# Segment sums of the SSD heads as differences of cumulated sums, in place of masked selects

## The chip, the cores and the metric

The kernel runs on one core of a Trainium2 chip. The metric is device time in microseconds (us) from the first to the last instruction with what lies around it, lower is better. Matmuls run on TensorE (PE; weight loads are listed apart as PEld), elementwise work on VectorE (DVE), ScalarE (ACT) and GpSimd (POOL); transfers are issued by SyncE (SP) unless said otherwise.

## What is computed

One layer of a hybrid block: adaLN-modulated norm, one input projection, an RG-LRU half and an SSD (Mamba-2) half, both bidirectional, an output projection with a residual, then a squared-ReLU MLP and a final norm. There are 1024 latent tokens and 256 context tokens of width 1024. The SSD half has 8 heads in 2 groups and works in chunks of 128 tokens. What matters here is the decay inside a chunk:

```python
a_cs = jnp.cumsum(A, axis=2)                      # A = dt * (-exp(a_log)), per chunk
seg_in = a_cs[:, :, :, None] - a_cs[:, :, None, :]
l_mat = jnp.exp(jnp.where(tri, seg_in, -jnp.inf))
y_diag = jnp.einsum('bclsg,bclsge,bcsgep->bclgep', cb, l_mat, X)
```

It is done once for each direction; the second direction runs over flipped tokens. In the kernel both directions share one matrix per head: entries with l >= s hold the forward decay, those below it the backward one.

## The kernel before

**Tiling.** Everything is float32 or float32r (split into a high and a low part where a product needs it). The input projection goes in 18 steps over tiles of 128 columns (`ORDER`), each step in pieces of 512, 512 and 256 tokens, each piece 8 k tiles of three products (`in_part`, lines 342 to 344). A tile framework orders the work: each engine gets a fixed list of instructions, made at build time from priorities, and semaphores do the rest. Pools hand out buffers by tag: `up` has 4 tiles of 512 columns, `gw` has 2 (`GW_N`), the heap `b` has 11 blocks of 1286 columns, the PSUM tag `a` has 2 banks.

**The segment sums.** `m_groups` is a generator that runs between the products of the projection: after each k tile of a piece of 512 tokens `in_part` takes one step of it (`tick`), from step 11 of the order (X1) on; what is left at the end of step 15 (lg1) is run off there. There are 16 groups: 8 chunks by 2 groups of four heads. For one group POOL makes four masked tiles `z` (line 777): the decays `a` of a token and head, high part and low part, forward and backward, spread over the 128 columns l and set to zero on one side of the diagonal. Four products (line 759) with strictly triangular matrices of ones, `gt_r` and `lt_r`, add them over the 128 tokens into one PSUM bank `sg`. Two `z` tiles exist, so POOL runs two products ahead at most. The generator takes 4 steps per group and 2 at the end, 66 in all of the 80 that steps 11 to 15 offer.

**What follows.** `m_group` makes `dd` on POOL (line 795, the difference of the two step sizes, masked), takes the exponential of `sg` on ACT into `gm` (lines 805 and 124, since the helper `tab` records it), then on DVE four times (dd + dt) * gm, one per head (line 807), and gm * C B^T (line 816), and stores the result to `m_dram` on SP (line 817). `dd` and `gm` are both tiles of the tag `up`. Much later `y_chunk` loads it again (line 827).

**What shares the stretch.** On DVE: the convolutions' three steps per tile (line 426), the adaLN sums (`ada2`, line 877, two per step), the low parts of the weights (line 138), gelu products (line 907). On ACT: evacuation of the projection's pieces (line 453) and of transposes (lines 622 and 624), first convolution taps (424), Silu and Gelu with loads of their tables (124). POOL also clears the pads of the convolution tiles (lines 407 to 412). After step 15 the states follow (`ssd_state`, lines 732 to 751, PSUM tag `a`).

**Set-up.** `ssd_dt` makes the step sizes and the decays `aneg`, their high and low parts (lines 688 and 689), and the cumulated sums for another purpose (`acsp`, lines 691 to 700).

Of the kernel before, what the change touches and what calls it, by code (L numbers as in the profile page):

```python
# [15 lines left out]
P = 128  # L16
# [9 lines left out]
# order of the input projection's column tiles: (kind, index)  # L26
# [11 lines left out]
# how far ahead of its place in the program the scheduler may take some work  # L38
EARLY, EARLY_W, EARLY_C, EARLY_G, EARLY_M, EARLY_L = 300, 400, 300, 50, 100, 200
EARLY_A, EARLY_B, EARLY_E, WO_E, WO_A = 100, 100, 100, 200, 200  # L40
# every N2_MOD-th tile of the second norm is modulated on VectorE, the others on ScalarE
N2_MOD = 12
# order of products 7 and 4 of the MLP's last matmul, and in the last chunk
# [4 lines left out]
# columns of the feature-major vector pack  # L48
# [3 lines left out]
# columns of the row pack  # L52
# [4 lines left out]
def kernel(  # L57
# [39 lines left out]
    y_dram = dram.tile([4, P, L], F32, name="y_dram")  # L97
    g1_dram = dram.tile([1, D], F32, name="g1_dram")
# [18 lines left out]
    gt_r = cst.tile([P, P], F32R, name="gt_r")  # L117
    lt_r = cst.tile([P, P], F32R, name="lt_r")
# [3 lines left out]
    def tab(out_, in_, func, chain=True, **kw):  # L122
        """An activation that needs its own table: these keep their order."""
# [16 lines left out]
    def softplus(out_, v, n, tmp):  # L140
        # max(v, 0) + log1p(exp(-|v|)), the logarithm as 2 atanh(w / (2 + w))
# [14 lines left out]
    with ExitStack() as mctx:  # L156
# [12 lines left out]

        def load_split(src, n, name, scale=None, row=None, nk=8):  # L170
            """k tiles of [128, n] weights as hi and lo parts; entry k gives (hi, lo)."""
# [22 lines left out]
        sil = cst.tile([P, 16], F32, name="sil")  # L194
        tab(sil, fmv[:, V_C : V_C + 16], AF.Silu)
        # per k: c_hi, cc_hi, c_lo, cc_lo; and c, cc, 0, 0 for the columns taken in float32
# [20 lines left out]
        def norm_x(g):  # L217
            lo_i, hi_i = groups[g]
            for i in range(lo_i, hi_i):
                junk = wq.tile([P, 1024], BF16, tag="gw", name=f"sq{i}", bufs=GW_N)  # L220
                act.activation(junk, xt[i][:, :D], AF.Square, accum_out=ss[:, i : i + 1])
# [43 lines left out]
        def ada1(b):  # L265
            """Shift and scale of feature tiles 2b and 2b + 1: [shift, shift, scale, scale] x (latents, context)."""
# [41 lines left out]
        # latents in two halves and the context: entry [g][k]  # L308
# [444 lines left out]
        def m_groups():  # L753
# [3 lines left out]
            def product():  # L757
# [6 lines left out]
                if d and part:  # L764
                    m_group(c, g, sg)
# [872 lines left out]
```

## Time and profile before

| | |
|---|---|
| median of 3 runs | 1209.3 us (1208.99 to 1215.41) |
| profiled execution, span | 1212.3 us; its own whole time is not given apart |
| PE, PEld busy | 1154.7 us (95%), 944.6 us (78%) |
| DVE, ACT, POOL busy | 916.9 us (76%), 648.7 us (54%), 80.8 us (7%) |

A share of busy time is an average over the span. Matmuls are pipelined, so that a matmul's busy time is longer than the time from its start to the start of the next. Where two engines use the same memory port an instruction lasts longer than alone; the shortest of a kind and its median then lie apart.

### The profile page before, as it was taken

To read this page: it belongs to the slowest core of one execution; us is meant where nothing else is said; L and a number is where in the kernel's file an instruction comes from. 1 tells how busy PE (TensorE), PEld (TensorE's weight loads), DVE (VectorE), ACT (ScalarE), POOL (GpSimd) and SP (SyncE) were. 2 spreads that over 40 slices of the span, in tenths; PEclk is the share of its full clock that TensorE was granted. 3 is DMA by queue.
4 is the path that set the end of the run, shared out by engine and by line. 5 is a ranking of instruction groups with operands and counts; after the bars stand their busy time and mean duration, and the time that the engine had idled before them with its cause. 6 is when DMAs were issued, how large, how long until landed. Compare 5 with 4: busy or idle time off the path is not lost.

```text
span 1212.3 us, 15731 instructions
## 1 busy us (share of the span) xinstructions
PE 1154.7 (95%) x5790; PEld 944.6 (78%) x5790; DVE 916.9 (76%) x1224; ACT 648.7 (54%) x1019; POOL 80.8 (7%) x120
## 2 busy tenths in 40 slices
PE   7899898998989999989899999999999999999997
PEld 2588787787767889988578777778878888888886
DVE  3775876888997698756996566656667787889996
ACT  5868377575555177527755455545574352333343
POOL 0000000004775000000000000000000000000000
PEclk9899998999999999999899999999999999999999
DMA  9621243223243256752285653545357444435403
GB/s 335 218 84 57 75 127 120 89 88 107 77 130 122 77 186 190 232 197 97 88 277 166 225 161 136 154 157 179 121 178 312 174 174 172 142 138 210 172 10 129
DMA packets 86480, 184.39 MB, mean 152 GB/s; under 512 B 8314, under 2 KB 19962, under 8 KB 82820
## 3 DMA queue, kind: packets, MB, share of 16 engines
q1 hardware_dynamic: 86404, 183.40, 44.9%
q8 instruction: 45, 0.74, 0.3%
q14 instruction: 31, 0.25, 0.1%
HBM read 133.03 MB, written 50.34 MB: 151 GB/s over the span
## 4 chain that ended last, share of the span: by engine, by line
PE 67%; DVE 14%; DMA 9%; ACT 4%; issue 3%; POOL 2%; SPq 1%; DVEq 0%; ACTq 0%; POOLq 0%
PE bx L1403 5%; PE bx L1402 5%; PE bx L1404 5%; DMA w1r<-in_w_dram 4%; PE x L1184 4%; PE x L1185 4%; PE x L1186 3%; PE bv L1403 2%; PE bv L1402 2%; PE bv L1404 2%; POOL z L777 2%; DMA ada2r<-in_ada_w_dram 1%; PE st L740 1%; PE v L1184 1%; PE v L1185 1%
## 5 line engine op out<-in xcount | busy, mean ns | idle before, releaser
L1184 PE MATMUL x<-hbh,wah 128*128 128x512 f32 x256 | 102.6, 401 | 6.6 <-DVE sv L1353 4.7
L1186 PE MATMUL x<-hbh,wal 128*128 128x512 f32 x256 | 101.4, 397 | 1.3 <-DVE wal L138 1.1
L1185 PE MATMUL x<-hbl,wah 128*128 128x512 f32 x256 | 101.4, 396 | 0.9 <-DVE hbl L138 0.9
L138 DVE TENSOR_TENSOR wal<-w1r,wah 128x512 fp32r<-128x512 f32 x64 | 44.0, 689 | 39.3 <-ACT wah L137 39.0
L137 ACT CAST wah<-w1r 128x512 fp32r<-128x512 f32 x64 | 39.5, 618 | 57.3 <-PE v L1185 30.3
L1184 PEld LDWEIGHTS x<-hbh,wah 128*128 128x128 f32 x256 | 48.6, 190 | 23.8 <-DVE sv L1353 8.7
L1186 PEld LDWEIGHTS x<-hbh,wal 128*128 128x128 f32 x256 | 48.7, 190 | 13.3 <-DVE wal L138 3.2
L1185 PEld LDWEIGHTS x<-hbl,wah 128*128 128x128 f32 x256 | 48.6, 190 | 11.6 <-DVE hbl L138 2.0
L124 ACT ACT_TABLE_LOAD x40 | 51.3, 1283 | 5.2 <-DVE gm L807 1.8
L1184 PE MATMUL v<-hbh,wah 128*128 128x512 f32 x128 | 50.4, 394 | 0.8 <-ACT wah L137 0.4
L1185 PE MATMUL v<-hbl,wah 128*128 128x512 f32 x128 | 50.2, 392 | 0.5 <-DVE hbl L138 0.5
L1186 PE MATMUL v<-hbh,wal 128*128 128x512 f32 x128 | 50.1, 391 | 0.4 <-DVE wal L138 0.4
L877 DVE SCALAR_TENSOR_TENSOR aacc<-ada2r,sil,aacc 128x512 f32<-128x512 f32 x48 | 39.5, 823 | 13.6 <-DMA ada2r<-in_ada_w_dram 13.5
L1429 DVE TENSOR_TENSOR acc<-acc,bx 128x512 f32<-128x512 f32 x52 | 35.4, 684 | 15.7 <-PE bx L1404 15.6
L777 POOL TENSOR_SCALAR_AFFINE_SELECT z<-a_hi 128x512 fp32r<-128x512 f32 x32 | 37.8, 1180 | 19.7 <-PE sg L759 17.8
L124 ACT ACTIVATE g<-gp,fmv 128x512 f32<-128x512 f32 (+1 forms) x48 | 28.7, 616 | 16.2 <-PE gp L503 15.8
L807 DVE SCALAR_TENSOR_TENSOR gm<-dd,dtv,gm 128x128 f32<-128x128 f32 x64 | 34.9, 591 | 2.8 <-issue 2.1
L137 ACT CAST wah<-sa 128x512 fp32r<-128x512 f32 x32 | 20.0, 624 | 28.0 <-PE x L1185 12.5
L1184 PEld LDWEIGHTS v<-hbh,wah 128*128 128x128 f32 x128 | 24.0, 188 | 7.3 <-ACT sp L1210 1.0
L1328 DVE TENSOR_TENSOR sa<-w1r,w1r 128x512 f32<-128x512 f32 x15 | 10.4, 692 | 24.6 <-DMA w1r<-in_w_dram 24.6
L1186 PEld LDWEIGHTS v<-hbh,wal 128*128 128x128 f32 x128 | 24.0, 188 | 6.1 <-DVE wal L138 1.2
L1185 PEld LDWEIGHTS v<-hbl,wah 128*128 128x128 f32 x128 | 24.0, 188 | 5.9 <-DVE hbl L138 1.1
(911 smaller groups left out, 3783.8 us busy)
## 6 DMA issues: line engine op xcount, KB each, us to landing
hr<-hs_dram SPq DMA_DIRECT2D x28, 1024.0 KB, 4.8
w1r<-in_w_dram SPq DMA_DIRECT2D x64, 256.0 KB, 4.0
hs_dram<-s SPq DMA_DIRECT2D x64, 256.0 KB, 3.0
w<-in_w_dram SPq DMA_DIRECT2D x16, 1024.0 KB, 5.5
ada2r<-in_ada_w_dram SPq DMA_DIRECT2D x48, 256.0 KB, 3.0
ada1r<-in_ada_w_dram SPq DMA_DIRECT2D x32, 256.0 KB, 4.2
hs_dram<-sp SPq DMA_DIRECT2D x32, 256.0 KB, 2.4
xt<-in_x_dram SPq DMA_DIRECT2D x8, 512.0 KB, 6.6
```

Of the source, the lines that this page charges most:

```text
L124: ins = act.activation(out_, in_, func, **kw).ins
L137: act.copy(hi, src)
L138: vec.tensor_sub(lo, src, hi.bitcast(F32))
L777: pool.affine_select(zt.rearrange("p (h l) -> p h l", h=4), src[:, c, hs].bitcast(F32).unsqueeze(2).to_broadcast([P, 4, P]), pattern=[[0, ...
L877: vec.scalar_tensor_tensor(acc, raw, sil[:, 2 * k : 2 * k + 1], acc, ALU.mult, ALU.add)
L1184: pe.matmul(ps, w[0][:, ks], hi[:, cs], start=(first and kk == 0), stop=False, **kw)
L1185: pe.matmul(ps, w[0][:, ks], lo[:, cs], start=False, stop=False, **kw)
L1186: pe.matmul(ps, w[1][:, ks], hi[:, cs], start=False, stop=(kk == 3), **kw)
L1402: pe.matmul(ps, h[0][:, hs], w[0][:, ws], start=(first and q == 0), stop=False, **kw)
L1403: pe.matmul(ps, h[0][:, hs], w[1][:, ws], start=False, stop=False, **kw)
L1404: pe.matmul(ps, h[1][:, hs], w[0][:, ws], start=False, stop=(q == 3), **kw)
L1429: vec.tensor_tensor(sl, sl, ps, ALU.add)
```

## The change

The four masked selects and four products of a group are replaced. `ssd_rows`, run at the end of `ssd_dt`, makes the cumulated sums of the latent chunks as rows: for each chunk, direction and head a row of 128 tokens, by two products that transpose and add at once. Its high and low parts go to `v_dram` with a row pitch of 1152, so that a read at pitch 512 finds each head's row in a column block of its own; the negated parts go to `s_dram`. For each group POOL loads 8 rows of each into one of four slots of 16 partitions, three groups ahead. The other 8 rows of each slot are constant: ones in `sgs`, and a pattern of ones in `sgv` that POOL makes before the first group. One product with 16 contraction rows for each direction then gives acs[l] - acs[s] for four heads, unmasked, in a bank of its own. The wrong side of the diagonal is positive there, so the minimum of the two directions selects the right one: ACT copies the first direction out of PSUM, DVE takes the minimum with the second, and ACT takes the exponential of that in place. The generator takes 5 steps per group, 2 for the last. The triangular matrices, their load and casts, `a_hi` and `a_lo` are gone. The two `gw` tiles of 512 columns become one of 1024.

```diff
@@ constants
-    gt_r = cst.tile([P, P], F32R, name="gt_r")
-    lt_r = cst.tile([P, P], F32R, name="lt_r")
+    sgs = cst.tile([P, 2, P], F32R, name="sgs")
...
-        tri = up("tri", n=256)
-        nc.sync.dma_start(tri, cst_in[:, 3:5, :].rearrange("p j m -> p (j m)"))
-        vec.tensor_copy(gt_r, tri[:, 0:P])
-        vec.tensor_copy(lt_r, tri[:, P : 2 * P])
+        for d in range(2):
+            pool.tensor_copy(sgs[:, d], ones)
@@ gate weights of the LRU
-            gh = wq.tile([P, 512], F32R, tag="gw", name=f"gh{f}", bufs=GW_N)
-            gl = wq.tile([P, 512], F32R, tag="gw", name=f"gl{f}", bufs=GW_N)
+            gw = gw_tile(f"gw{f}")
+            gh, gl = gw[:, :512], gw[:, 512:]
@@ ssd_dt
-            vec.tensor_copy(a_hi, aneg)
-            vec.tensor_sub(a_lo, aneg, a_hi.bitcast(F32))
...
+            ssd_rows()
+
+        def ssd_rows():
+            az = up("az")
+            azv = az.rearrange("p (v c j) -> p v c j", v=4, c=NT)
+            vec.memset(az[:, 0 : 2 * P], 0.0)
+            for d in range(2):
+                vec.tensor_copy(azv[:, d, :, 8 * d : 8 * d + 8], aneg[:, :NT, 8 * d : 8 * d + 8])
+            ps = psp.tile([P, 512], F32, tag="p", name="acsr")
+            pe.matmul(ps[:, :P], az[:, 0:P], tri_le, start=True, stop=False)
+            pe.matmul(ps[:, :P], az[:, P : 2 * P], tri_ge, start=False, stop=True)
+            vt, st = blk("vrow", F32R), up("srow", F32R)
+            vec.memset(vt[:, 0:1152].bitcast(F32), 0.0)
+            vh, vl = vt[:, 0:P], vt[:, 512 : 512 + P]
+            act.copy(vh, ps[:, :P])
+            vec.tensor_sub(vl, ps[:, :P], vh.bitcast(F32))
+            act.activation(st[:, 0:P], vh.bitcast(F32), AF.Identity, scale=-1.0)
+            act.activation(st[:, P : 2 * P], vl.bitcast(F32), AF.Identity, scale=-1.0)
+            nc.sync.dma_start(v_dram.rearrange("(p m) -> p m", m=1152), vt[:, 0:1152].bitcast(F32))
+            nc.sync.dma_start(s_dram.rearrange("(p m) -> p m", m=256), st[:, 0:256].bitcast(F32))
@@ m_groups
-            for c in range(NT):
-                for g in range(2):
-                    for d in range(2):
-                        for part, src in ((0, a_hi), (1, a_lo)):
-                            if len(todo) == GW_N:
-                                product()
...
-                            pool.affine_select(
...
+            todo = [(c, g) for c in range(NT) for g in range(2)]
+            def load(n):
...
+                o = 32 * (n % 4)
+                sv = v_dram.rearrange("(c d g m) -> c g d m", d=2, g=2, m=4608)[c, g, :, 0:4096]
+                pool.dma_start(sgv[o : o + 8], sv.rearrange("d (k m) -> k d m", k=8))
+                ss_ = s_dram.rearrange("(c d g k m) -> c g k d m", d=2, g=2, k=8, m=P)[c, g]
+                pool.dma_start(sgs[o + 8 : o + 16], ss_)
+            sgv = gw_tile("sgv").rearrange("p (d m) -> p d m", d=2)
+            for o in range(0, P, 32):
+                pick = ident[o : o + 16, o + 8 : o + 16].rearrange("p (h r) -> p h r", r=2)
+                for d in range(2):
+                    pool.tensor_tensor(
...
+            for n in range(3):
+                load(n)
+            for n, (c, g) in enumerate(todo):
+                o = 32 * (n % 4)
+                load(n + 3)
+                sg = []
+                for d in range(2):
+                    sg.append(a_ps(f"sg{c}{g}{d}"))
+                    ins = pe.matmul(
+                        sg[d], sgs[o : o + 16, d], sgv[o : o + 16, d], start=True, stop=True
+                    ).ins
+                    if after[0] is not None:
+                        order(ins, after[0])
+                    yield
+                m_group(c, g, sg)
+                for _ in range(3 if n < len(todo) - 1 else 0):
+                    yield
@@ m_group
-            tab(gm.rearrange("p h l -> p (h l)"), sg, AF.Exp, chain=False)
+            gf = gm.rearrange("p h l -> p (h l)")
+            act.copy(gf, sg[0])
+            vec.tensor_tensor(gf, gf, sg[1], ALU.min)
+            tab(gf, gf, AF.Exp, chain=False)
```

## Rows read from the trace of the kernel before

**Rows 1.** The page: span, busy time and share of each engine.

```profile
span 1212.3 us, 15731 instructions
PE 1154.7 (95%) x5790; PEld 944.6 (78%) x5790; DVE 916.9 (76%) x1224; ACT 648.7 (54%) x1019; POOL 80.8 (7%) x120
```

**Rows 2.** Busy time by stretch: us, PE, PEld, DVE, ACT, POOL, clock, DMA.

```profile
239.00:289.00 50.00, 48.59 (x259) 40.40 (x259) 42.15 (x43) 33.11 (x43) 3.41 (x15) 0.97 0.29 92
...
288.70:391.00 102.30, 92.17 (x459) 71.98 (x458) 95.72 (x128) 59.99 (x93) 76.19 (x84) 1.00 0.32 105
```

**Rows 3.** Waits, 288.7 to 391: who for whom, us, times, longest.

```profile
POOL z L777 <- PE sg L759: 20.5, 16, 7.0
...
PEld sg L759 <- POOL z L777: 16.4, 19, 1.7
PE sg L759 <- POOL z L777: 8.7, 13, 1.3
```

**Rows 4.** The chain of waits of the same stretch, by line.

```profile
by line: POOL z L777 22.5%; PE sg L759 8.3%; DVE gm L807 7.7%; DVE v L426 5.5%; issue 4.6%; POOL dd L795 4.1%; PE lg1p L342 3.7%; PE lg1p L344 3.6%; PE lg1p L343 3.6%; PE X3p L343 3.2%; PE X3p L344 3.2%; PE X3p L342 3.0%; PE X1p L344 2.8%; 
```

**Rows 5.** L759 in the stretch (PE, PEld); then PE's timeline: start, us, instruction.

```profile
288.70:391.00 102.30, 27.22 (x64) 11.93 (x64) 1.00 0.32 105
...
341.76 0.40 PE L343 MATMUL X3p<-al,wX3h 128*128 128x512 f32 x1
341.99 0.40 PE L344 MATMUL X3p<-ah,wX3l 128*128 128x512 f32 x1
343.66 0.50 PE L759 MATMUL sg<-z,lt_r 128*128 128x512 f32 x1 [1.27 <-POOL z L777]
```

**Rows 6.** Timeline of DVE and POOL side by side.

```profile
338.71 1.92 DVE L426 SCALAR_TENSOR_TENSOR v<-X2p,fmv,v 128x1282 f32<-128x1282 f32 x1
339.25 1.88 POOL L777 TENSOR_SCALAR_AFFINE_SELECT z<-a_lo 128x512 fp32r<-128x512 f32 x1
```

**Rows 7.** Single lines: shortest/median/longest ns, first and last start.

```profile
L426 DVE SCALAR_TENSOR_TENSOR u<-lx2p,fmv,u x3: 1551/1551/1553, 166.0 to 169.9; 128x1282 f32<-128x1282 f32 x3
...
L807 DVE SCALAR_TENSOR_TENSOR gm<-dd,dtv,gm x64: 339/715/731, 296.1 to 386.0; 128x128 f32<-128x128 f32 x64
...
L816 DVE TENSOR_TENSOR gm<-gm,cb x16: 676/691/1118, 299.3 to 386.4; 128x512 f32<-128x512 f32 x16
...
L877 DVE SCALAR_TENSOR_TENSOR aacc<-ada2r,sil,aacc x48: 741/752/1125, 56.5 to 355.3; 128x512 f32<-128x512 f32 x48
...
L777 POOL TENSOR_SCALAR_AFFINE_SELECT z<-a_lo x32: 637/683/1884, 242.7 to 379.2; 128x512 fp32r<-128x512 f32 x32
```

**Rows 8.** DVE's busy time in the stretch, of L426, L807, L877, L816, in order.

```profile
288.70:391.00 102.30, 27.32 (x15) 1.00 0.32 105
...
288.70:391.00 102.30, 34.87 (x64) 1.00 0.32 105
...
288.70:391.00 102.30, 12.17 (x12) 1.00 0.32 105
...
288.70:391.00 102.30, 13.31 (x16) 1.00 0.32 105
```

**Rows 9.** Prices: single lines, a group with mean ns, L817's landing, one group's timeline.

```profile
L1429 DVE TENSOR_TENSOR acc<-acc,bx x52: 670/682/689, 956.9 to 1205.5; 128x512 f32<-128x512 f32 x52
...
L453 ACT COPY X1p<-X1p 128x512 f32<-128x512 f32 x2 | 1.2, 590 | 4.8 <-PE X1p L344 4.8
...
L124 ACT ACTIVATE gm<-sg x16: 587/599/657, 292.5 to 384.6; 128x512 f32<-128x512 f32 x16
...
DMA to landing us min/median/max: 2.0/2.6/3.1
...
299.63 0.60 ACT L124 ACTIVATE gm<-sg 128x512 f32<-128x512 f32 x1
...
312.31 0.68 DVE L816 TENSOR_TENSOR gm<-gm,cb 128x512 f32<-128x512 f32 x1
```

**Rows 10.** Price of the set-up: one DVE line, as in rows 7.

```profile
L872 DVE MEMSET aacc<- x6: 485/485/485, 1.2 to 315.9; 128x512 f32 x6
```

More of the change, by code (lines that the diff above doesn't have):

```diff
@@ L97 @@
     y_dram = dram.tile([4, P, L], F32, name="y_dram")
+    v_dram = dram.tile([P * 1152], F32, name="v_dram")
+    s_dram = dram.tile([P * 256], F32, name="s_dram")
     g1_dram = dram.tile([1, D], F32, name="g1_dram")
@@ L168, in up, with gw_tile @@
             return wq.tile([P, 512], dt, tag="up", name=name, bufs=4)[:, :n]
+        def gw_tile(name, dt=F32R):
+            return wq.tile([P, 1024], dt, tag="gw", name=name)
         def load_split(src, n, name, scale=None, row=None, nk=8):
@@ L219, in norm_x @@
             for i in range(lo_i, hi_i):
-                junk = wq.tile([P, 1024], BF16, tag="gw", name=f"sq{i}", bufs=GW_N)
+                junk = gw_tile(f"sq{i}", BF16)
                 act.activation(junk, xt[i][:, :D], AF.Square, accum_out=ss[:, i : i + 1])
@@ L666 @@
         aneg = cst.tile([P, NCH, 16], F32, name="aneg")
-        a_hi = cst.tile([P, NCH, 16], F32R, name="a_hi")
-        a_lo = cst.tile([P, NCH, 16], F32R, name="a_lo")
         nea = cst.tile([P, 16], F32, name="nea")
@@ L753, in m_groups @@
         def m_groups():
-            todo = []
-            def product():
-                (c, g, d, part), sg, zt = todo.pop(0)
-                ins = pe.matmul(
-                    sg, (gt_r, lt_r)[d], zt, start=(d == 0 and part == 0), stop=(d == 1 and part == 1)
-                ).ins
-                if after[0] is not None:
-                    order(ins, after[0])
-                if d and part:
-                    m_group(c, g, sg)
-            for c in range(NT):
-                for g in range(2):
-                    for d in range(2):
-                        for part, src in ((0, a_hi), (1, a_lo)):
-                            if len(todo) == GW_N:
-                                product()
-                            if d == 0 and part == 0:
-                                sg = a_ps(f"sg{c}{g}")
-                            hs = slice(8 * d + 4 * g, 8 * d + 4 * g + 4)
-                            zt = wq.tile([P, 512], F32R, tag="gw", name=f"z{c}{g}{d}{part}", bufs=GW_N)
-                            pool.affine_select(
-                                zt.rearrange("p (h l) -> p h l", h=4),
-                                src[:, c, hs].bitcast(F32).unsqueeze(2).to_broadcast([P, 4, P]),
-                                pattern=[[0, 4], [1 - 2 * d, P]],
-                                compare_op=ALU.is_ge,
-                                fill=0.0,
-                                base=0,
-                                channel_multiplier=2 * d - 1,
-                            )
-                            todo.append(((c, g, d, part), sg, zt))
-                            yield
@@ L788, in m_groups @@
-            while todo:
-                product()
-                yield
+            todo = [(c, g) for c in range(NT) for g in range(2)]
+            def load(n):
+                if n >= len(todo):
+                    return
+                c, g = todo[n]
+                o = 32 * (n % 4)
[3 more added lines that the diff above has]
+                pool.dma_start(sgs[o + 8 : o + 16], ss_)
@@ new lines, in m_groups @@
+            sgv = gw_tile("sgv").rearrange("p (d m) -> p d m", d=2)
[3 more added lines that the diff above has]
+                    pool.tensor_tensor(
+                        sgv[o : o + 16, d].rearrange("p (h l) -> p h l", h=4),
+                        pick[:, :, 0:1].to_broadcast([16, 4, P]),
+                        pick[:, :, 1:2].to_broadcast([16, 4, P]),
+                        ALU.add,
+                    )
```

## The prediction

> **What bounds the kernel now.** I read the busy shares first: TensorE's matmuls cover 95% of a span of 1212.3 us, VectorE (DVE) 76%, GpSimd (POOL) 7% [rows 1]. So TensorE time that goes mostly comes back, unless another engine fills the place. POOL's 80.8 us lie almost wholly in one stretch, and all that the change rewrites after its set-up lies there too, so that stretch is read alone: 288.7 to 391.0 us, from the first segment-sum product to the end of the step that holds the last. In its 102.3 us PE is busy 92.17, DVE 95.72, ACT 59.99, POOL 76.19, at a granted clock of 1.00 throughout (the upper level, 2.4 GHz) [rows 2]. DVE, not PE, is the fullest engine.
>
> The waits of the stretch [rows 3] say who holds whom. PE's products and their weight loads wait for POOL's selects (8.7 and 16.4 us), and POOL waits for PE to free one of the two `z` tiles (20.5 us): a ring of two buffers. The chain of waits of the stretch alone gives POOL's `z` selects 22.5%, the most of all [rows 4].
>
> Why is POOL slow? A select lasts 0.64 us at its shortest [rows 7]. Side by side with DVE [rows 6] one lasts 1.88 and the convolution step next to it 1.92, where the same shape on `u`, far from POOL's work, took 1.55. L807 takes 0.339 or about 0.715 [rows 7]. Each holds the other up. So the selects cost twice: PE waits for them, and DVE is stretched by them.
>
> **The change, part by part.**
>
> *PE.* A product of 512 columns is busy 0.39 to 0.50 us, but the next one starts 0.23 us later [rows 5], so 0.23 is its price. 64 such products [rows 5] become 32 with 16 contraction rows. No row shows that height with 512 columns; a full one is the upper bound, none the lower, and I take 0.23, since in [rows 5] products of other kinds with 512 columns keep the same step. Gain 32 x 0.23 = 7.4 us (14.7 at the far bound). The stall: 8.7 us as PE's idle time is the lower bound, 8.7 + 16.4 = 25.1 the upper, which counts many waits twice. In [rows 5] an idle of 1.27 cost 343.66 - (341.99 + 0.23) = 1.44, or 0.17 more than shown; 13 such waits make 8.7 + 13 x 0.17 = 10.9. I take 11. PE alone would need 102.3 - 7.4 - 11 = 84 us.
>
> *DVE.* What POOL now adds: L426 27.32 - 15 x 1.55 = 4.1; L807 34.87 - 64 x 0.339 = 13.2; L877 12.17 - 12 x 0.741 = 3.3; L816 13.31 - 16 x 0.676 = 2.5 [rows 7, 8]. Together 23.1 us. 64 of POOL's 80 selects go and the 16 `dd` selects stay, so I take 0.8 of it: 18.4. New are 16 minima, 128x512 with one operand from PSUM; the same form at L1429 takes 0.682 [rows 9], so 10.9 us. DVE: 95.7 - 18.4 + 10.9 = 88.2 us. Bounds: 83.5 if all 23.1 go, 97.4 if the 32 new POOL transfers hold DVE up as selects did (48 of 80 left, 9.2 off).
>
> *ACT.* 16 copies PSUM to SBUF more, 0.59 each by L453 [rows 9]: 9.4 us, to 69.4 of the stretch, hidden. What isn't hidden is the new wait: the exponential follows the copy in ACT's order and waits for DVE's minimum. Queued behind it on ACT are the evacuations of the projection's pieces (L453) and of the transposes (L622, L624), for which PE waits in turn. On DVE the first L807 of a group waits for the exponential.
>
> *PE's new wait.* A group now takes both banks of the `a` tag. The first product of the next group waits for ACT's copy, the second for DVE's minimum, and behind them stand the projection's products. Before, a bank came back after the exponential and two groups were in flight; now it is one.
>
> *POOL's queue.* Per group one `dd` select and two transfers (8 rows of 4 KB and 8 rows of 1 KB). The trace has no transfer issued by POOL: its nearest rows are a select alone, 0.64 us, and one held up, 1.88 [rows 6, 7], and the true price may lie under the first. The refill of a slot waits for the product of the group before, and behind it stand the `dd` select and the pad memsets. With a period of 102.3 / 16 = 6.4 us and three groups loaded ahead there are 19 us to cover a landing; the stores of 256 KB here land in 2.0 to 3.1 us [rows 9]. I take no exposed wait. Without that cover, about 3 us a group, 48 in all.
>
> *The sum of the stretch.* DVE is busy 94% of it now (95.72 / 102.3). With the new order copy, minimum, exponential, L807 it won't be fuller by much; at 94 to 97% the 88.2 us need 91 to 94, and PE's 84 fit under that. I take 92.5, or -9.8 us. What is late next is DVE, not POOL.
>
> *Set-up.* `ssd_rows` follows `ssd_dt`, long before the stretch: two memsets of 1152 and 256 columns at 0.485 per 512 [rows 10], 1.3 us, two small copies, a subtraction of 128 columns for which the nearest row is L807's 0.34 [rows 7], less the two small operations that made `a_hi` and `a_lo`. About +1.3 us on DVE, three short ACT operations, two small products, two stores on SP. No chain hangs on them before 289, so 0 to 1.3. `vrow` takes one of the heap's 11 blocks for some us, which may hold back an LRU block. The eight pattern sums on POOL fall where its first selects ran, at 242 us [rows 7], beside a DVE that is busy 42.15 of 50 us [rows 2]; each may add 1.92 - 1.55 = 0.37, so 0 to 3.0. One load and two casts at the start fall away and are hidden on DVE. I take +1.0 for all (0 to 4.3).
>
> *Total.* -9.8 + 1.0 = -8.8 us. Against the profiled execution that makes a span of 1203.5. That span, 1212.3, is 3.0 above the median of the three runs, 1209.3, and its own whole time can't be less; I carry the difference over to the median: **1200.5 us**.
>
> **The rivals.**
>
> *A, the forecast:* DVE sets the stretch at 91 to 94; with 0 to 4.3 for the set-up 1198 to 1205.
>
> *B, both fall:* the transfers cost DVE nothing and the order leaves no gaps, so PE's 84 us decide: -18.3 + 1.0, 1192. For it: DVE's 83.5 then fits. Against: two engines within 1 us of each other would have to run without gaps, with one group in flight.
>
> *C, POOL's transfers take the selects' place:* DVE needs 97.4, at 97% 100.4: -1.9 + 1.0, 1208.4. For it: any POOL work that touches memory beside DVE has cost it in this stretch. Against: transfers of 8 rows are not 128 rows of arithmetic. The Trainium skill, in "SBUF — State Buffer", section "Who interferes with whom", says that a DVE instruction with two SBUF inputs contends with a GpSimd instruction that reads SBUF, and not with one that only writes it. By that rule issuing loads would cost DVE nothing and the sum would be 88.2 or less, never 97.4; the trace agrees as far as selects go (L807, two SBUF inputs, 0.339 against 0.715), and no run here shows a transfer from POOL beside DVE, so C keeps a chance.
>
> *D, slower: the hand-over of a group becomes the ring.* The place is the `up` tag, four buffers, two per group, and the order copy, minimum, exponential, four L807, L816, store. The copy of group n needs the buffer whose store belongs to group n-2. Undisturbed: 0.59 + 0.68 + 0.60 + 4 x 0.34 + 0.68 + 2.6 = 6.5 us for two groups, harmless. But in the trace the second group's exponential starts at 299.63 and its L816 at 312.31 [rows 9], 12.7 us, with convolution steps and weight splits between. From exponential to the end of L816 that group takes 13.4 us, the last one 386.4 + 0.7 - 384.6 = 2.5 [rows 7, 9]. If the middle of the two, 8.0, is the rule, then with 1.3 for copy and minimum, 1.9 for a convolution step ahead of the minimum [rows 6] and 2.6 for the store, two groups take 13.8, the 16 take 110, and the stretch is 8 us longer: 1209.3 + 8 + 1 = 1218. It decides as soon as the loop passes 2 x 6.4 = 12.8 us. Against: those delays come mostly from a DVE that is 94% busy and stretched by 23 us that now go.
>
> *E, it doesn't do what it says early:* the heap block or the pattern sums hold back the LRU tail, the full 4.3 us and some more, which leaves about -4: 1205.
>
> **How the numbers follow.** A 0.56, B 0.09, C 0.13, D 0.15, E 0.07. The likeliest is A, 1200.5 us, its own range 1198 to 1205. Half of a per cent, 6.0 us, is about what a measurement of this kernel can tell from no change, so faster is under 1203.3, slower over 1215.3. Faster: 0.52 of A and B's 0.09, 0.61. Same: the rest of A, C, E, and the mild end of D, 0.27. Slower: 0.12 of D. The range takes in most of B and the mild part of D: 1190 to 1212.
>
> **What would show it.** Right: the 32 products wait for no select; L807 falls from 34.87 / 64 = 0.54 each towards 0.37 to 0.42, L816 from 0.83 towards 0.70; 16 minima at 0.68; the stretch takes 91 to 94 us with DVE 94% busy or more; PE's remaining waits at the products name DVE's minimum or ACT's copy. B: PE over 97% busy there. C: L807 still near 0.54, beside long POOL transfers. D: copies or exponentials wait for a landing of `m_dram`, and DVE falls under 90%. Wrong altogether: products that wait for POOL's transfers, PE waiting for transposes' evacuations behind a held exponential, or a loss that lies before 289 us or after 391, where ssd_state follows without the fourteen quiet steps that it has now.

## The result, and the profile after

| | before | after |
|---|---|---|
| median | 1209.3 us (1206.8 to 1215.4, 5 runs) | 1219.7 us (1218.5 to 1220.5, 5 runs) |
| ratio to before | 1 | 1.0077, 95% interval 1.0057 to 1.0097 |
| span of the profiled execution | 1212.3 us | 1217.1 us |
| first segment-sum product to first y product | 289.0 to 422.7: 133.7 us | 289.6 to 432.0: 142.4 us |

The forecast was 1200.5 us; the change makes the kernel slower by about 9.3 us by the ratio (0.77% of 1209.3; the two medians lie 10.4 apart). The last row of the table is the measure used from here on: PE's first start of tile `sg` to its first start of `yd`, where the y stage takes over. Three traces of the kernel before or nearly so (before, b0 and e16 below) gave 133.7, 133.8 and 134.3, so it is steadier than whole spans. (The profiled execution of before lies near the top of its runs, which is why the spans differ by less than the medians.)

The page of after, busy time and chain:

```profile
PE 1161.1 (95%) x5762; PEld 943.4 (78%) x5762; DVE 906.1 (74%) x1241; ACT 663.4 (55%) x1041; POOL 43.7 (4%) x98
...
PE 78%; DVE 10%; DMA 6%; ACT 3%; issue 2%; SPq 0%; DVEq 0%; ACTq 0%
```

Against [rows 1], DVE and POOL lost work as forecast, and PE, which has 32 products fewer, is busier. Groups of DVE and POOL, 289 to 403 us (busy, mean ns of one, then idle time before them and its releaser):

```profile
L836 DVE SCALAR_TENSOR_TENSOR gm<-dd,dtv,gm 128x128 f32<-128x128 f32 x64 | 18.7, 344 | 10.1 <-ACT gm L126 10.0
L845 DVE TENSOR_TENSOR gm<-gm,cb 128x512 f32<-128x512 f32 x16 | 11.7, 733 | 0.2
L833 DVE TENSOR_TENSOR gm<-gm,sg 128x512 f32<-128x512 f32 x16 | 10.9, 681 | 0.4 <-PE sg L808 0.4
...
L785 POOL DMA_DIRECT2D sgs<-s_dram x12 | 6.6, 552 | 0.0
L783 POOL DMA_DIRECT2D sgv<-v_dram x12 | 6.6, 551 | 44.6 <-PE sg L808 44.6
```

L836 is the old L807: 18.7 us instead of 34.87 [rows 8]. The minimum costs 0.681, as priced. POOL waits 44.6 us for PE to free a slot and nobody waits for its transfers. So the gain on DVE came, and DVE stands idle 10 us for the exponential. Busy time by stretch (us, PE, PEld, DVE, ACT, POOL, clock):

```profile
300.00:330.00 30.00, 30.00 (x171) 24.02 (x170) 22.41 (x37) 19.13 (x30) 6.00 (x15) 1.00 0.28 92
330.00:360.00 30.00, 30.00 (x146) 22.38 (x145) 25.55 (x42) 21.73 (x37) 7.47 (x13) 1.00 0.42 139
360.00:371.00 11.00, 11.00 (x49) 7.88 (x49) 7.26 (x15) 7.62 (x14) 2.35 (x4) 1.00 0.36 124
371.00:385.10 14.10, 10.13 (x21) 5.82 (x22) 7.41 (x17) 7.07 (x10) 3.86 (x6) 0.64 0.18 62
```

At first PE is full and DVE at 66 to 85%, the other way round from [rows 2]. Then, from 371 to 385, PE is busy 72% of the time, DVE 53% and ACT 50%, and the granted clock is 0.64 on average. Two readings follow, one for each part.

**PE while it is full: the 16-row product.** PE's timeline around one (start, busy time):

```profile
299.87 0.39 PE L348 MATMUL X1p<-al,wX1h 128*128 128x512 f32 x1
300.10 0.40 PE L349 MATMUL X1p<-ah,wX1l 128*128 128x512 f32 x1
300.43 0.49 PE L808 MATMUL sg<-sgv,sgs 16*128 16x512 f32 x1
300.85 0.50 PE L347 MATMUL X1p<-ah,wX1h 128*128 128x512 f32 x1
301.19 0.39 PE L348 MATMUL X1p<-al,wX1h 128*128 128x512 f32 x1
301.42 0.40 PE L349 MATMUL X1p<-ah,wX1l 128*128 128x512 f32 x1
```

The steps are 0.33, 0.42 and 0.34 where three usual ones are 0.23 each: 1.09 - 0.69 = 0.40 us more for each product. At 0.40 each, 32 of them cost about 12.8 us, against the 7.4 that 32 products fewer were to save.

**PE while it waits: the hand-over.** The third group's second product starts at 303.14. What DVE does until its minimum (L833), and ACT from its copy (L832) to its exponential (L126, tile `gm`):

```profile
308.25 1.55 DVE L429 SCALAR_TENSOR_TENSOR v<-X0p,fmv,v 128x1282 f32<-128x1282 f32 x1
310.91 0.69 DVE L140 TENSOR_TENSOR wX3l<-wX3r,wX3h 128x512 fp32r<-128x512 f32 x1 [1.11 <-ACT wX3h L139]
311.52 1.55 DVE L429 SCALAR_TENSOR_TENSOR v<-X0p,fmv,v 128x1282 f32<-128x1282 f32 x1
312.98 0.68 DVE L140 TENSOR_TENSOR wlg0l<-wlg0r,wlg0h 128x512 fp32r<-128x512 f32 x1
313.58 1.55 DVE L429 SCALAR_TENSOR_TENSOR v<-X0p,fmv,v 128x1282 f32<-128x1282 f32 x1
...
315.38 0.68 DVE L833 TENSOR_TENSOR gm<-gm,sg 128x512 f32<-128x512 f32 x1
```

```profile
311.26 0.59 ACT L832 COPY gm<-sg 128x512 f32<-128x512 f32 x1
...
318.58 0.59 ACT L456 COPY X2p<-X2p 128x512 f32<-128x512 f32 x1 [2.14 <-PE X2p L349]
319.19 1.28 ACT L126 ACT_TABLE_LOAD   x1
320.48 0.63 ACT L126 ACTIVATE gm<-gm 128x512 f32<-128x512 f32 x1
```

Product 303.1, copy 311.3, minimum 315.4, exponential 320.5. Each step stands in its engine's fixed list behind other work, the minimum behind convolution steps and weight splits, the exponential behind the evacuation of a piece of X2 that PE hadn't finished. The banks come back with the ends of copy and minimum, at 311.9 and 316.1; the next two products start at 312.2 and 317.4. By the end of lg0 (363.0, against 377.2 before) the projection is 14 us ahead, but the groups aren't: the 19th of 32 products starts at 359.9. Of the rest nine crowd into lg1 (363.2 to 388.3) and four come later, among the products of lg2. The last product starts at 398.9, before at 380.7.

What follows the last product is bounded by another engine than before. Before, the projection ends at 422.5 and the first y product starts at 422.7, PE being busy without a break; after, the projection ends at 423.5 and the first y product starts at 432.0, with DVE full, mostly of the states' steps. From the last product to the first y product are 31 to 36 us in every run of the changed kernel, and 42 in the kernel before. The stretch before the y stage, before and then after:

```profile
390.00:420.00 30.00, 30.00 (x133) 24.36 (x132) 22.33 (x37) 2.40 (x4) 0.00 (x0) 1.00 0.29 97
```

```profile
403.00:432.00 29.00, 25.23 (x109) 19.46 (x109) 27.96 (x47) 7.87 (x17) 0.00 (x0) 1.00 0.43 154
```

### The profile page after: what moved, and what is told of

Same layout as the page of the kernel before. It is cut to its first block, busy times and chain, and to the rows that moved or that the text cites. A ratio compares the mean times of both kernels' runs of the same rounds, so it can differ in the third digit from the quotient of the medians.

```text
span 1217.1 us, 15740 instructions
## 1 busy us (share of the span) xinstructions
PE 1161.1 (95%) x5762; PEld 943.4 (78%) x5762; DVE 906.1 (74%) x1241; ACT 663.4 (55%) x1041; POOL 43.7 (4%) x98
## 4 chain that ended last, share of the span: by engine, by line
PE 78%; DVE 10%; DMA 6%; ACT 3%; issue 2%; SPq 0%; DVEq 0%; ACTq 0%
PE bx L1432 5%; PE bx L1433 5%; PE bx L1431 5%; PE x L1213 5%; PE x L1214 4%; PE x L1215 4%; PE bv L1432 2%; PE bv L1433 2%; PE bv L1431 2%; PE v L1213 2%; PE v L1214 2%; DMA w1r<-in_w_dram 2%; PE v L1215 2%; PE ada L282 1%; PE yd L858 1%
## 5 line engine op out<-in xcount | busy, mean ns | idle before, releaser
L906 DVE SCALAR_TENSOR_TENSOR aacc<-ada2r,sil,aacc 128x512 f32<-128x512 f32 x48 | 38.3, 797 | 10.4 <-DMA ada2r<-in_ada_w_dram 10.1
L126 ACT ACTIVATE g<-gp,fmv 128x512 f32<-128x512 f32 (+1 forms) x48 | 28.3, 616 | 19.4 <-PE gp L506 19.2
L836 DVE SCALAR_TENSOR_TENSOR gm<-dd,dtv,gm 128x128 f32<-128x128 f32 x64 | 18.7, 344 | 10.1 <-ACT gm L126 10.0
L1221 ACT ACTIVATE sp<-sp 128x512 f32<-128x512 f32 x32 | 20.2, 631 | 10.0 <-DVE sp L1398 9.6
L1215 PE MATMUL y<-hbh,wal 128*128 128x512 f32 x64 | 25.0, 391 | 0.0
```

Of the source, the lines that this page charges most:

```text
L126: ins = act.activation(out_, in_, func, **kw).ins
L906: vec.scalar_tensor_tensor(acc, raw, sil[:, 2 * k : 2 * k + 1], acc, ALU.mult, ALU.add)
L1215: pe.matmul(ps, w[1][:, ks], hi[:, cs], start=False, stop=(kk == 3), **kw)
L1221: act.activation(t, src, AF.Relu)
```

## The experiments

All times are medians of 4 to 12 runs (b0 and e14 have one run each); ratios are to runs of the kernel before on the same chip, with their 95% interval. The two theories after the first reading were S (the shape of the product) and H (the late hand-over); a third, E (the set-up), came from the first eight runs.

| run | us | ratio | first product to first y product |
|---|---|---|---|
| after | 1219.7 | 1.0077 (1.0057 to 1.0097) | 142.4 |
| e2_rows128 | 1211.4 | 0.9997 (0.9977 to 1.0017) | 135.3 |
| e1_two_exps | 1210.0 | 0.9981 (0.9958 to 1.0004) | 134.2 |
| e5_prio | 1211.2 | 0.9986 (0.9963 to 1.0009) | 133.8 |
| e7_one_dir | 1196.8 | 0.9869 (0.9832 to 0.9905) | 118.2 |
| e8_prio_rows128 | 1202.7 | 0.9938 (0.9918 to 0.9958) | 124.3 |
| e9_pair | 1214.4 | 1.0022 (1.0003 to 1.0040) | 136.8 |
| e10_prio_pair | 1205.6 | 0.9946 (0.9929 to 0.9964) | 128.4 |
| b0_before | 1210.8 | one run | 133.8 |
| e11_all3 | 1204.6 | 0.9935 (0.9915 to 0.9955) | 125.5 |
| e12_prio_pair_act | 1207.5 | 0.9965 (0.9947 to 0.9983) | 128.5 |
| e13_full128 | 1202.7 | 0.9918 (0.9892 to 0.9944) | 126.7 |
| e14_rows64 | 1212.8 | one run | 134.0 |
| e15_before_rows | 1219.0 | 1.0053 (1.0037 to 1.0069) | 140.2 |
| e16_before_prio | 1212.1 | 0.9999 (0.9983 to 1.0014) | 134.3 |
| e17_prio_min | 1213.8 | 1.0012 (0.9997 to 1.0026) | 137.4 |
| e18_prio_act | 1217.1 | 1.0046 (1.0030 to 1.0062) | 139.3 |
| e19_own_tile | 1215.8 | 1.0034 (1.0018 to 1.0051) | 140.1 |
| e20_full128_own | 1200.8 | 0.9918 (0.9894 to 0.9942) | 123.5 |

### The shape alone

```diff
-                        sg[d], sgs[o : o + 16, d], sgv[o : o + 16, d], start=True, stop=True
+                        sg[d], sgk, ag[0][0][0], start=True, stop=True
```

`sgk` is a constant tile of 128x128.

> The 32 products take 128 contraction rows of constant operands (weights of zero) in place of the 16 loaded rows; loads, copies, minima and exponentials stay. Left out: the segment sums themselves, so every decay is 1. Theory S (the 16-row shape costs: from the changed kernel's trace about 0.63 us a product with its neighbours, in place of 0.23) expects the step back at 0.23, some 32 x 0.40 = 12.8 us of TensorE time back, and 1207 us. Theory H (the hand-over of one group at a time, from bank to copy to minimum to exponential, sets when the last group ends) expects the step at 0.23 too, but the last product still at 396 us or later and a time of 1215 to 1220.

1.0077 to 0.9997: 0.0080, or 9.7 us of 1209.3. That lies between the 1207 of S and the 1215 to 1220 of H: the shape costs much of the loss, and not all. The last product starts at 392.4, earlier than the 396 that H expected. This run also takes away the products' dependence on the loaded rows; e14 and e8 below both do without it and differ by the height alone.

### The hand-over: the same result with other work, one direction, or only another order

```diff
 e1_two_exps
-            act.copy(gf, sg[0])
-            vec.tensor_tensor(gf, gf, sg[1], ALU.min)
-            tab(gf, gf, AF.Exp, chain=False)
+            tab(gf, sg[0], AF.Exp, chain=False, scale=0.1)
+            tab(gn, sg[1], AF.Exp, chain=False, scale=0.1)
+            vec.tensor_tensor(gf, gf, gn, ALU.min)
 e7_one_dir (the same three lines of m_group become one)
-                for d in range(2):
+                for d in range(1):
...
+            tab(gf, sg[0], AF.Exp, chain=False, scale=0.1)
 e5_prio: the three lines of the changed kernel, under
+            with tc.high_priority(offset=EARLY):
```

> ACT takes the exponential of both banks straight out of PSUM, into two tiles, and DVE takes the minimum after it, in SBUF: no engine goes back and forth, and ACT alone frees both banks. Left out: the true decay (the exponentials are taken of a tenth of their argument, to stay finite). Also two buffers of 512 columns in place of three of 264 for the token-major z tiles, which could cost a little before 170 us. H expects the last product at 385 us or earlier, in place of 399, and 1205 to 1212 us. S expects no change from the changed kernel, 1217 to 1221 us, since the 32 products keep their shape.

> The changed kernel with copy, minimum and exponential of a group put 300 places ahead of their place in the program, as the evacuations of the projection's pieces are; the same work, another order on ACT and DVE. H expects that copies and minima stand directly behind their products, the last product before 390 us, and 1205 to 1214 us. S expects 1217 to 1221 us.

> Only the forward product of each group, with its exponential straight from the bank: no copy, no minimum, one bank a group as before the change, the same pace of 5 steps a group. Left out: the backward direction and the true decay (a tenth of the argument). H expects the last product at 380 us or earlier and 1195 to 1203 us. S expects half the products' price back, 16 x 0.63 = 10 us: 1209 us, with PE's time and not the chain as the cause.

All three came out in the range that H gave, though e1's last product started at 391.9, not by 385. e5 changes no work at all, only its place in the lists (`EARLY` is 300 places), and gains 0.0091, 11.0 us; its clock in the stretch is 1.00 throughout. It keeps the pace of five steps a group, so the quiet steps (steps of the generator that issue nothing) that the change uses up don't explain these 11 us. Much of the gain is seen in the step of lg1, which takes 25.1 us in after (363.2 to 388.3) and 16.4 in e5 (363.6 to 380.0): after's has 4.0 us of idle PE between 371 and 385.1, and by an estimate 3.8 us of low clock, since 15 products of lg1 and two of `sg` take 8.5 us from 376.75 to 385.26 where 15 x 0.23 + 2 x 0.63 makes 4.7. e7 takes away half the products, the copy, the minimum and the second bank at once and so can't tell S from H; it shows what lies in the two together, 0.0208 or 25 us.

### Do they add?

```diff
 e8_prio_rows128: both edits, of e5 and e2
 e9_pair: in m_groups
                     if after[0] is not None:
                         order(ins, after[0])
-                    yield
+                yield
                 m_group(c, g, sg)
-                for _ in range(3 if n < len(todo) - 1 else 0):
+                for _ in range(4 if n < len(todo) - 1 else 1):
 e10_prio_pair: both edits, of e5 and e9
```

> Both single repairs at once: the group's copy, minimum and exponential are taken up to 300 places ahead of their place in the program, and the 16-row segment-sum products are replaced by products of 128 rows on constant operands (the segment sums are left out, so the decay is 1). Alone each gave about 10 us against the changed kernel (1211.2 and 1211.4). Theory S (the 16-row shape costs TensorE some 0.3 us at each change of shape) and theory H (the hand-over of a group is late) are two causes that add: 1200 to 1204 us, last segment-sum product some 92 to 95 us after the first, y stage no later than 131 us after the first product. Rival: both only remove the same slack, one chain with one length: 1208 to 1212, like either alone.

> The two 16-row products of a group follow each other directly, and the quiet steps between groups are kept, so that TensorE changes shape twice in a group where it changed four times; nothing else is changed. Theory S: a product of 16 rows behind another of 16 rows costs the usual 0.23 us, so some 0.3 to 0.4 us a group is saved, 5 to 6 us in all: 1214 to 1217 (the changed kernel stands near 1221 against this kernel before). If the cost sits in every 16-row product, whatever its neighbour: 1219 to 1222. Theory H alone: the second product now waits in front of the projection for the second bank, 1219 to 1224.

> Early hand-over and adjacent pair together, with the whole computation kept. If S and H add and a pair saves 5 to 6 us: 1205 to 1208 us, which would be under the kernel before (near 1211 here). If only the order counts: 1210 to 1212. If the adjacent pair makes TensorE stand for the second bank: 1213 to 1218.

> The kernel before once more, for a second trace of it. If the 3 us by which the first segment-sum product of the changed kernel starts later are scatter, it starts here anywhere from 285 to 292 us; the stretch from it to the last product should again be 95 us within 1, and to the y stage 137 within 1.5. If they belong to the set-up of the change, it starts here at 285 to 286 again.

They add, within the intervals: e8 gains 0.0139 (16.8 us) where each alone gave 0.0080 and 0.0091, and its 124.3 us are 9.4 less than before. In it PE, not DVE, is full from the first product to the last:

```profile
292.30:380.20 87.90, 87.27 (x458) 72.05 (x456) 78.18 (x135) 68.68 (x108) 12.62 (x20) 1.00 0.39 129
```

e9 came out in the range of S, but not by S. Of 16 pairs only three are adjacent in its trace (starts 0.33 to 0.34 us apart); for the others PE's list has products of the projection between the two, though the edit puts them side by side in the program (that the list was made so because the second bank comes free late is argued, not shown). One that is adjacent:

```profile
296.13 0.40 PE L349 MATMUL X1p<-ah,wX1l 128*128 128x512 f32 x1
296.45 0.73 PE L808 MATMUL sg<-sgv,sgs 16*128 16x512 f32 x2
297.11 0.50 PE L347 MATMUL X1p<-ah,wX1h 128*128 128x512 f32 x1
297.45 0.40 PE L348 MATMUL X1p<-al,wX1h 128*128 128x512 f32 x1
```

From 296.13 to 297.45 is 1.32 us with two of them in it, four usual steps are 0.92: a pair costs 0.40 once, so three pairs save 1.2 us of the 6.7 gained. The rest isn't the shape: the last product starts at 396.6 instead of 398.9, the y stage at 427.6 instead of 432.0, and the y stage itself (first to last start of `yd`) takes 64.5 us instead of 66.9, at a clock of 1.00 where after stands at 0.50 for 10.3 us. That the clock makes those 2.4 us is argued, since the y stage before took 67.7 at 1.00. e10 is faster than both kernels. b0's first product started at 286.1, where before's started at 289.0, so this start moves by 3 us from run to run. The 95 and 137 us in b0's text aren't what before's trace gives (91.7 to the last product, 133.7 to the y stage); b0 gave 91.7 and 133.8.

### The rows of the pattern, and the height

```diff
 e11_all3, e12_prio_pair_act (on e8, e10)
-                    pool.tensor_tensor(
+                    act.copy(
                         sgv[o : o + 16, d].rearrange("p (h l) -> p h l", h=4),
-                        pick[:, :, 0:1].to_broadcast([16, 4, P]),
-                        pick[:, :, 1:2].to_broadcast([16, 4, P]),
-                        ALU.add,
+                        pks[o : o + 16].unsqueeze(2).to_broadcast([16, 4, P]),
                     )
 e13_full128 (on e12): one slot of 128 rows, all but 16 of them zero
-                        sg[d], sgs[o : o + 16, d], sgv[o : o + 16, d], start=True, stop=True
+                        sg[d], sgs[:, d], sgv[:, d], start=True, stop=True
...
+                load(n + 1)
                 yield
 e14_rows64 (on e8)
-                        sg[d], sgk, ag[0][0][0], start=True, stop=True
+                        sg[d], sgk[:64], ag[0][0][0][:64], start=True, stop=True
```

> The kernel with early hand-over and 128-row products (1202.7 us; segment sums left out, the decay is 1), and with one edit more: the eight pattern sums of the set-up are copied by ACT from a small table instead of being added on POOL. In every trace of the changed kernel these eight take 1.43 us each on POOL beside a full DVE, whose steps next to them are longer than in the kernel before (a convolution step 1.80 against 1.55, a weight split 1.10 against 0.59, a modulation product 0.99 against 0.80), and the fourth projection piece that follows takes 22 to 25 us against 21. Theory E (these sums cost DVE, and DVE the projection): those durations fall back to the values before, and 3 to 4 us are won: 1198.5 to 1200.5 us, which would be the forecast with every cause of the loss removed. Rival: the late start of the stretch is scatter, 1202 to 1204.

> The same single edit (pattern copies on ACT in place of pattern sums on POOL) on the kernel with early hand-over and adjacent pair, the whole computation kept; that kernel took 1205.6 us. Theory E: 1201.5 to 1203.5 us, first segment-sum product 2 to 4 us earlier than 290, the rest of the stretch as it was. Rival (scatter): 1205 to 1207.

> The whole computation kept, with products of 128 rows: one slot, its 16 rows of data above 112 rows of zeros, in place of four slots of 16 rows; early hand-over, adjacent pair and pattern copies on ACT as in the run before it. Theory S: a product costs 0.23 us wherever it stands, and some 5 us of the 32 x 0.39 that the shape costs come back: 1197 to 1200 us. Against it: the next group's rows can only be loaded after the products of this one, some 0.55 us of issue for each of two transfers and 2 to 3 us of landing against a period of 6 us. If that cover is too thin, products wait for transfers and it takes 1203 to 1210.

> The kernel with early hand-over and products of constant operands once more, with 64 rows in place of 128 (segment sums left out, the decay is 1). One look, for the distance of starts around such a product: if the height of 16 is what costs, the steps are 0.23 us as with 128 rows; if any product that isn't of the full height costs a change of shape, they are 0.33 before it, 0.42 after it and 0.34 behind that, as with 16 rows.

The pattern sums did stretch DVE's steps, and the time didn't follow. One step of each trace, 225 to 275 us, first after, then e12:

```profile
L906 DVE SCALAR_TENSOR_TENSOR aacc<-ada2r,sil,aacc 128x512 f32<-128x512 f32 x8 | 8.0, 994 | 2.0 <-DMA ada2r<-in_ada_w_dram 1.9
```

```profile
L908 DVE SCALAR_TENSOR_TENSOR aacc<-ada2r,sil,aacc 128x512 f32<-128x512 f32 x8 | 6.0, 749 | 4.0 <-DMA ada2r<-in_ada_w_dram 3.9
```

DVE's relief became its own idle time; e12's first product starts 2.4 us earlier than e10's, and still e11 and e12 are no faster than e8 and e10 (0.9935 against 0.9938, 0.9965 against 0.9946). This form of E fell. e13 keeps the whole computation and gives 0.9918, wholly under e12's interval. It also makes two pattern copies instead of eight. At 1202.7 us it misses its 1197 to 1200, and its products wait 1.2 us for transfers, so the thin cover costs little; they keep the usual step:

```profile
318.60 0.40 PE L352 MATMUL X2p<-ah,wX2l 128*128 128x512 f32 x1
318.83 0.39 PE L802 MATMUL sg<-sgv,sgs 128*128 128x512 f32 x1
319.06 0.40 PE L350 MATMUL X2p<-ah,wX2h 128*128 128x512 f32 x1
```

With 64 rows (e14) they don't, so it isn't the height of 16 as such. The height is all that differs from e8, and the stretch is 134.0 us instead of 124.3, 9.7 more (one run):

```profile
298.20 0.39 PE L351 MATMUL X1p<-ah,wX1l 128*128 128x512 f32 x1
298.52 0.49 PE L810 MATMUL sg<-ah,sgk 64*128 64x512 f32 x1
298.94 0.50 PE L349 MATMUL X1p<-ah,wX1h 128*128 128x512 f32 x1
299.28 0.39 PE L350 MATMUL X1p<-al,wX1h 128*128 128x512 f32 x1
```

### Controls on the kernel before, and the links one by one

```diff
 e15_before_rows (kernel before): ssd_rows and its two stores, read by nobody
             vec.tensor_tensor(ddt, dtv[:, :NT, 0:8], dtv[:, :NT, 8:16], ALU.subtract)
+            ssd_rows()
 e16_before_prio (kernel before)
+            with tc.high_priority(offset=EARLY):
                 tab(gm.rearrange("p h l -> p (h l)"), sg, AF.Exp, chain=False)
 e17_prio_min (changed kernel)
+            with tc.high_priority(offset=EARLY):
                 vec.tensor_tensor(gf, gf, sg[1], ALU.min)
 e18_prio_act (changed kernel): the same line over the copy, and over the exponential
 e19_own_tile (changed kernel), e20_full128_own (on e13)
+        srow = cst.tile([P, 256], F32R, name="srow")
-            az = up("az")
+            az = srow.bitcast(F32)
-            vt, st = blk("vrow", F32R), up("srow", F32R)
+            vt, st = blk("vrow", F32R), srow
```

> The kernel before with its group's exponential taken up to 300 places ahead, as the copy, minimum and exponential were in the run that gained 11 us. Theory H (three dependent steps in the static order of two engines are the new cost, where before there was one): the kernel before gains little, 1208 to 1212.5. Rival: early hand-over removes slack that both kernels have, so it gains about as much here, 1200 to 1205.

> The changed kernel with only DVE's minimum taken ahead. Full early hand-over took 0.9986 of the kernel before, none 1.0077. If the minimum's place behind convolution steps on DVE is the late link: at most 1.000, some 1209 to 1212 us. If ACT's copy and exponential are: 1.005 or more, 1217 to 1222.

> The changed kernel with only ACT's copy and exponential taken ahead, DVE's minimum in its old place. If DVE's minimum is the late link: 1.005 or more, 1217 to 1222 us. If ACT's two steps are: at most 1.000, 1209 to 1212. If each is late on its own, both this run and the one with the minimum alone lie between, near 1.004.

e16 is the control for H: the kernel before gains nothing (0.9999), so the 11 us are a cost that the change brought, not slack that both have (the kernel before has only one such step to take ahead). The minimum's place on DVE is worth 0.0065 (7.9 us), that of ACT's two steps 0.0031 (3.7 us); together 0.0096, about e5's 0.0091. e17 lies just over its bound of 1.000 and e18 just under its 1.005, and both intervals take in the bounds. So it is shown that DVE's link weighs more; that ACT's is late on its own rests on a gain of 0.0031 whose own interval nearly reaches zero.

> The kernel before with the new row set-up alone added behind the step sizes (two memsets, two small products, the copies, the subtraction, the two stores); nothing reads what it stores. If this set-up is what delays the stretch: 3 to 6 us slower, 1214 to 1218 against 1212 for the kernel before, first segment-sum product at 288 us or later. If it is hidden, as I priced it (0 to 1.3 us): 1211 to 1213, first product at 282 to 286.

> The changed kernel, its row set-up in a buffer of its own (1 KB a partition) in place of two of the four shared ones; nothing else differs. The changed kernel is 1.0077 of the kernel before, and the row set-up alone cost 0.0053. If it is the borrowed buffers (in two traces a split waits 1.2 and 2.8 us for the store of the negated rows): 1.002 to 1.005, some 1214 to 1218 us, and no wait for that store. If it is the work itself, or the new order of everything behind it: 1.006 to 1.009.

> The fastest kernel so far with the whole computation kept (products of 128 rows, early hand-over, adjacent pair, pattern copies on ACT: 1202.7 us, 0.9918), its row set-up in a buffer of its own. If the borrowed buffers cost: 0.987 to 0.990, 1197 to 1200 us. If not: 0.991 to 0.993, as before.

The row set-up alone makes the kernel before slower by 0.0053, 6.4 us; its 1219.0 us lie over the 1214 to 1218 expected. Its cost isn't seen where it stands (145 to 150 us) but mostly later: its first product starts at 291.1 (289.0, 286.1 and 288.5 without it), and from there to the y stage are 140.2 us for 134. All of that lies between the first and the last product (98.1 us for 91.7): POOL's selects wait 40.0 us for PE there instead of 20.5, and the granted clock is 0.83 in 322 to 332 and in 362 to 372, where before's is 1.00. Whether these are cause or consequence isn't shown. One wait on the way is plain, from DVE's waits of e15, 130 to 195 us:

```profile
DVE aacc L900 <- DMA ada2r<-in_ada_w_dram: 4.7, 3, 2.3
DVE ul L140 <- DMA s_dram<-srow: 2.8, 1, 2.8
```

The split of an LRU activation needs one of the four `up` tiles, and that tile is free only when the store of the negated rows has landed. With a buffer of its own (e19) that wait is gone and the changed kernel gains 0.0043, 5.2 us, in the range expected of the borrowed buffers. But in after the wait was only 1.2 us. In e13 it was 3.2, and in the fastest kernel the same edit, which takes that wait away too, gave nothing that can be told from zero (e20, 0.9918 like e13, four runs each). So the set-up's cost is shown, and e19's gain; that the borrowed buffers are the reason isn't, since the edit also moves the stores (from 150.5 to 154.1 us for the second) and with them perhaps the order behind them. How the cost reaches the stretch 140 us later, and why the fastest kernel doesn't gain, stays open. More tiles of the tag `up` or a third bank, which would lengthen the ring itself, weren't tried.

## Why the prediction was wrong, and where it was right

**PE's term failed.** "I take 0.23" for the 16-row product, with a full product as "the upper bound". No row showed that height, and here a shorter product isn't bounded by a full one: between full ones it costs 0.23 + 0.40. 32 of them at 0.63 are 20.2 us against 64 x 0.23 = 14.7, so the term is 5.4 lost, not 7.4 won; taking the shape away won 9.7 us. The Trainium skill, in "TensorE: Matmul & The Clock Gate", section "Why this matters for your kernels", says that a single product of 32 rows takes the same time as one of 128. No run here has one alone; between full products the rows here show otherwise, and the measurement decides.

**The bound was named wrong.** "DVE sets the stretch at 91 to 94" took DVE to be the fullest engine afterwards. DVE's own sum was good: 117.9 us busy before in 289.0 to 422.7, 111.0 after in 289.6 to 432.0, 6.9 less where 95.7 - 88.2 = 7.5 was forecast. But with it and the waits for selects gone PE is the bound, 100% until 371 us in after and 99% in e8 with DVE at 89%. That was rival B's bound without B's price.

**Rival D was the mechanism, at a wrong link.** "The hand-over of a group becomes the ring" had a chance of 0.15 and 1218 us. The ring is there and costs 11 us (e5, with e16 as its control). It isn't closed by the landing of `m_dram`, which D made its sign: ACT's copies waited for that 1.6 us once. D's other sign, DVE under 90%, did come (73.5 of 100.4 us from 289.6 to 390). The ring is closed by the static lists of DVE and ACT (e5, e17 and e18) and by the two banks of the `a` tag (read from the starts above, not tested), which stand in the prediction under "PE's new wait" without a price. That D's 1218 lies near the 1219.7 measured is luck: its sum has the wrong link, and neither the shape nor the set-up. The argument against D ("those delays come mostly from a DVE that is 94% busy and stretched") fell: DVE was relieved in full and the delays stayed, since they are places in a list, not lack of time.

**The set-up was under-priced.** "No chain hangs on them before 289, so 0 to 1.3", +1.0 in all and 4.3 at most; it costs 6.4 alone in the kernel before. The heap block was named as a risk, the two `up` tiles weren't looked at.

**Right:** the relief of DVE (L836 at 0.344 instead of 0.54; of the 18.4 us taken about 6.9 + 10.9 = 17.8 came), the minimum at 0.68 and ACT's copies at 0.59, POOL's transfers (0.55 us each, landing 1.9 to 3.8 us after issue, and no product waits for one). So C was wrong. By the rule of the Trainium skill that was cited there ("SBUF — State Buffer", "Who interferes with whom") transfers issued by POOL shouldn't hold DVE up, and the trace agrees: 0.344 each with 24 transfers in the same stretch, and four of them in 1.14 us (371.59 to 372.73) while POOL issues two.

**The sum of the parts.** With the shape and the hand-over repaired, the stretch is 9.4 us shorter (e8), where the forecast had 9.8; so its size was that of a kernel without the two costs it had not priced. That the two figures agree so well is in part luck: the forecast had DVE as the bound at 94 to 97%, and in e8 it is PE at 99%. The parts on record: shape 9.7, hand-over 11.0, both 16.8 (less than their sum, 20.7; that the two share some slack is argued, not shown), set-up 6.4 measured in another kernel. They aren't a complete account of every microsecond.

## What to carry to other kernels

Before work is taken off an engine to make room, ask what the fullest engine will be afterwards, and price its new instructions in their neighbourhood: a product of another height between full ones cost 0.63 us here, not 0.23, and one padded with zeros to 128 rows cost PE the usual 0.23. Where one dependent step became three on two engines, the places in the static lists decided, not the busy shares; try giving the chain priority, and test that on the old kernel too. Set-up can cost far from where it stands: here 6.4 us alone, most of it seen 140 us later.

## What the runs showed of the hardware

- A change of the number of contraction rows costs time on TensorE in both directions: steps of 0.33, 0.42 and 0.34 instead of 0.23, the same for 16 and for 64 rows.
- Two 16-row products on different rows start together (one such pair in after's trace). There the second product of one group and the first of the next, which lie in different slots, are recorded as one line of two with 0.50 us from the first start to the last end, about what one alone is busy (0.49):

```profile
327.88 0.28 PE L349 MATMUL X2p<-a,wX2l 128*128 128x256 f32 x1
328.09 0.50 PE L808 MATMUL sg<-sgv,sgs 16*128 16x512 f32 x2
328.52 0.39 PE L347 MATMUL X2p<-a,wX2h 128*128 128x256 f32 x1
```

- After the change the clock stands at 0.50, the lower level of 1.2 GHz, in two stretches around which before was at 1.00 (2.4 GHz), from 288.7 to 391 [rows 2] and from 390 to 450. Ahead of the first PE had stood twice: 1.65 us before 373.46 for ACT's copy of a group, and 2.08 us before 376.75 for the Gelu of lg0, which ACT did behind a group's exponential and a load of a table. Ahead of the second it was busy 25.2 of the 29 us from 403 to 432, in the state stage, which only lg3's products fill now (before, those of lg2 and lg3). In the second the clock is low although PE is busy all the time. Both stretches of after, then before:

```profile
374.90:385.10 10.20, 8.35 (x17) 5.21 (x18) 4.89 (x11) 5.28 (x7) 2.75 (x4) 0.50 0.10 35
432.90:443.20 10.30, 10.30 (x51) 10.30 (x51) 7.05 (x10) 7.27 (x22) 0.00 (x0) 0.50 0.24 72
```

```profile
420.00:450.00 30.00, 28.34 (x187) 25.40 (x185) 25.96 (x41) 22.23 (x52) 0.00 (x0) 1.00 0.54 172
```
